# A hybrid diffusion layer on one core: casts bound behind other work, and unread products laid on TensorE

## The chip, the cores and the metric

The kernel runs on one core of a Trainium2 chip. Its engines are TensorE (PE; its weight loads are PEld), VectorE (DVE), ScalarE (ACT), GpSimd (POOL) and SyncE (SP), which issues most of the DMAs. Each engine works through its own queue in order; semaphores hold an instruction until what it reads is written and what it overwrites has been read. The metric is the device time of one execution in microseconds, as the median of several runs. All times here are microseconds.

## The reference

One layer with 512 latent tokens (x) and 256 context tokens (ctx), width 1024, all float32:

```python
def hybrid_layer(...):
    x = ffn_sublayer(x, mod_x, 0, ffn1_w_in, ffn1_w_out)        # SwiGLU, hidden 2816
    ctx = ffn_sublayer(ctx, mod_c, 0, ffn1_w_in, ffn1_w_out)
    qa, ka, va, qkv_b, z_b, a_b, b_b, ga, gb = split_proj(modulate(x, shift_x, scale_x) @ w_in)
    ...
    o_a = na_latent(grid(qa), grid(ka), grid(va), kc_h, vc_h, na_rpb)   # neighbourhood attention, 8 heads of 64
    o_ctx2, s_ctx = gated_delta_chunks(..., s0, update_ctx)             # gated DeltaNet, 4 heads of 128, both ways
    o_lat2, _ = gated_delta_chunks(..., s_ctx, True)
    o_b = gdn_output(o_lat2[0] + jnp.flip(o_lat2[1], axis=2), z_b, gdn_norm_w)
    y = sigmoid(ga) * (o_a @ w_pa) + sigmoid(gb) * (o_b @ w_pb)
    x = post_ln(DEEPNORM_ALPHA * x + gate_x * (y @ w_o), ln_g[1], ln_b[1])
    x = ffn_sublayer(x, mod_x, 2, ffn2_w_in, ffn2_w_out)
    return x
```

`ffn_sublayer` is a layer norm with a modulation, `(silu(a) * b) @ w_down` with `a, b = u @ w_up`, a gate and a layer norm behind it. The modulations come from `silu(c) @ w_ada`. The DeltaNet solves a triangular system for each chunk of 64 tokens and then carries a state from chunk to chunk.

## The kernel before

**Products.** Float32 is kept by splitting. Each weight tile of 128x1024 is copied by ScalarE into a high part of a shorter type (`S.copy`, L135, shown as CAST), and VectorE subtracts it to get the low part (L137); both are in `split`. Activations are split in the same way (uxh and uxl for x, uch and ucl for the context, oah and oal for what attention gives). One product is three matmuls: high by high, low by high and high by low (`mm3k`, L190 to L192; `down`, L209, for the second matrices). `Stream` (`ws` for most weights, `wso` for w_o) loads weight tiles ahead in the order of use and splits them; its dictionary `behind` can name, for the tile of a given number, two instructions behind which its cast and its subtraction are put.

**Order.** The kernel is built in program order, and a scheduler then orders each engine's queue by a simulated timeline (`schedule_with_timeline_sim=True`). `tc.issue_after(i)` binds the instructions made inside it to come after instruction `i` in the order. So a new instruction or a new bond can move others far away from it.

**PSUM.** TensorE writes to 8 banks. Pools name the places in them: in the first FFN the pool `pp1` has a ring "ps" of 8 places; then come `pm` (3 places) and `pg` (5), whose tiles lie on the same banks, later others. A tile on a bank waits until the last reader of the tile that was there has read it.

**Stages.** In order of time:
- Start (0 to about 40): the modulation columns are worked out by VectorE (L279) as the ada weights arrive; `modulate_k` (from L348) transposes the normed x for one block k of 128 columns (L360), and the first three FFN units add their products to six "acc" places (L413 to L415) as each k becomes ready. `spread_crow` (L290) lays the vector c over the partitions with two products ahead of that.
- First FFN, to about 607. Behind it `u2` (through `to_u`, L146 transposes, L149 reads) makes the modulated tokens; the context's second tile, `u2(fc, pp, "c", 1, ys[1])`, is the last work in pool `pp1`.
- w_in, to about 818: units that each make one projection (`units`), in pools `pm` and `pg`.
- DeltaNet, to about 1000: `grams(0)`, `grams(1)`, the block inverses `inv_of` (L857 products of 32x32 and 64x64 on T, which SyncE loads at L976 from the row that `base_inverse` wrote) and the scans. TensorE has fills from w_in beside them until these run out.
- Attention, to about 1095: four units m of two heads each, each of four blocks b (`attend`). A block is scores sc (L1240), softmax (VectorE, ScalarE's exponent at L1248, POOL's scaling of pr at L1251), transposes pt (L1255), ScalarE's copies pT (L1257) and the products po with the values (L1266). `att_load(p, m)` loads qa, ka and kc of unit m, casts them on ScalarE (L1169) and has POOL subtract (L1170). It is called for unit m+1 as unit m is made, and units m and m+2 share their places. Products with w_pb lie between.
- The gates (L1330 on): eight tiles of w_pa (`gated`), each followed by a gate and a split of yb into yh and yl; w_o's tiles are cast and subtracted meanwhile. Then w_o, and the second FFN: four units, each over half of the tokens in two passes (`for i in range(2)`), then products of half the size, and the end at 1528.8.

## Time and profile before

| | us |
|---|---|
| median of 3 runs | 1526.87 |
| the three runs | 1526.37 to 1531.96 |
| profiled execution | 1530.66 |
| its span | 1528.8 |
| TensorE busy in it | 1462.6 |
| VectorE busy | 1050.0 |
| ScalarE busy | 605.4 |
| POOL busy | 226.8 |

The profiled execution is one more execution with a recorder; its time is 1.9 us longer than its span. It lies 3.79 above the median of the runs, between the fastest and the slowest of the three. The mean granted clock of TensorE over the span is 0.988. In a row of the timeline the columns are the start, the time from the first instruction's start to the last one's end, the engine, line and operation, what it writes and reads, and in brackets the idle time of the engine just before and what ended it.

### The profile page before, as it was taken

The page shows a single profiled execution, that of the slowest core. Times are in us where ns is not written, and L with a number is a line of the kernel's source. Part 1 is how long each engine was busy: PE and PEld are TensorE (multiplying, and loading weights), DVE is VectorE, ACT ScalarE, POOL GpSimd, SP SyncE. Part 2 cuts the span into 40 slices and gives each one's busy share as a digit, 9 for nine tenths or more (in the row PEclk, how much of TensorE's full clock was granted, in tenths as well). Part 3 has the DMA queues.
Part 4 walks back from the last instruction along what each step waited for, and adds up shares of the span by engine and source line. Part 5 has one row for each costly group of instructions (what it writes and reads, how often), then busy time and mean ns, then how long its engine had stood idle before and what let it go on. Part 6 is the DMA issues. An engine that isn't in the chain of part 4 may idle for free.

```text
span 1528.8 us, 23646 instructions
## 1 busy us (share of the span) xinstructions
PE 1462.6 (96%) x9221; PEld 1258.7 (82%) x9221; DVE 1050.0 (69%) x1792; ACT 605.4 (40%) x1005; POOL 226.8 (15%) x224
## 2 busy tenths in 40 slices
PE   6999999999999999999996899999999999999997
PEld 4779988888888887889875778867678999998886
DVE  8765942597554587768777895576669699886426
ACT  5444221322222255546543444266416444344310
POOL 0000000000000011323301001366421022220001
PEclk9999999999999999999998999999999999999999
DMA  9665742667454334222476634283353143333422
GB/s 370 207 237 180 222 142 97 211 213 260 168 192 146 130 112 137 87 90 79 141 216 180 172 99 122 69 284 117 91 174 138 56 139 102 106 110 139 138 83 83
DMA packets 107586, 230.72 MB, mean 151 GB/s; under 512 B 34177, under 2 KB 47825, under 8 KB 107473
## 3 DMA queue, kind: packets, MB, share of 16 engines
q1 hardware_dynamic: 105312, 221.79, 44.7%
q10 hardware_dynamic: 1586, 5.32, 0.9%
q0 software_dynamic: 576, 2.10, 0.4%
q8 instruction: 72, 1.18, 0.3%
q14 instruction: 40, 0.33, 0.1%
HBM read 206.33 MB, written 22.85 MB: 150 GB/s over the span
## 4 chain that ended last, share of the span: by engine, by line
PE 76%; DVE 10%; DMA 7%; issue 3%; ACT 2%; POOL 2%; SPq 0%; DVEq 0%; ACTq 0%; POOLq 0%
PE ps L209 19%; PE ps L190 8%; PE ps L192 8%; PE ps L191 8%; PE pm L190 5%; PE pm L192 5%; PE pm L191 5%; PE pc L857 2%; PE ps L1478 2%; PE ps L1480 2%; PE ps L1479 2%; DVE wl L137 2%; PE po L1266 1%; DMA T<-rd 1%; PE pt L1255 1%
## 5 line engine op out<-in xcount | busy, mean ns | idle before, releaser
L137 DVE TENSOR_TENSOR wl<-wr,wh 128x1024 fp32r<-128x1024 f32 (+1 forms) x215 | 263.0, 1228 | 195.1 <-ACT wh L135 194.3
L135 ACT CAST wh<-wr 128x1024 fp32r<-128x1024 f32 (+1 forms) x215 | 217.8, 1018 | 333.4 <-PE ps L209 105.0
L192 PE MATMUL ps<-uxh,wl 128*128 128x512 f32 (+1 forms) x496 | 179.6, 363 | 2.2 <-DVE wl L137 2.2
L191 PE MATMUL ps<-uxl,wh 128*128 128x512 f32 (+1 forms) x496 | 179.3, 363 | 0.8 <-DVE uxl L137 0.8
L190 PE MATMUL ps<-uxh,wh 128*128 128x512 f32 (+1 forms) x496 | 179.6, 365 | 0.0
L279 DVE SCALAR_TENSOR_TENSOR adap<-wr,crow 128x1024 f32<-128x1024 f32 x112 | 136.8, 1221 | 38.5 <-DMA wr<-in_w_adaT_dram 37.1
L112 POOL TENSOR_TENSOR rs<-ve,mhalf 128x1 f32<-128x1 f32 (+2 forms) x46 | 50.4, 1099 | 744.6 <-DVE ve L108 735.4
L190 PE MATMUL pm<-uxh,wh 128*128 128x512 f32 x320 | 133.0, 416 | 4.1 <-ACT spill L609 2.1
L192 PE MATMUL pm<-uxh,wl 128*128 128x512 f32 x320 | 128.2, 401 | 0.7 <-DVE wl L137 0.7
L191 PE MATMUL pm<-uxl,wh 128*128 128x512 f32 x320 | 127.8, 399 | 0.0
L192 PEld LDWEIGHTS ps<-uxh,wl 128*128 128x128 f32 x496 | 93.7, 189 | 17.9 <-DVE wl L137 3.3
L191 PEld LDWEIGHTS ps<-uxl,wh 128*128 128x128 f32 x496 | 94.0, 189 | 14.9 <-DVE uxl L137 1.0
L190 PEld LDWEIGHTS ps<-uxh,wh 128*128 128x128 f32 x496 | 93.4, 189 | 14.3 <-issue 0.8
L190 PE MATMUL ps<-uch,wh 128*128 128x256 f32 x352 | 98.6, 280 | 0.0
L192 PE MATMUL ps<-uch,wl 128*128 128x256 f32 x352 | 98.3, 279 | 0.0
L191 PE MATMUL ps<-ucl,wh 128*128 128x256 f32 x352 | 98.2, 279 | 0.0
L209 PE MATMUL ps<-wh,hx 128*128 128x512 f32 x352 | 94.8, 389 | 0.0
L209 PEld LDWEIGHTS ps<-wh,hx 128*128 128x128 f32 x352 | 65.9, 188 | 13.6
L190 PEld LDWEIGHTS pm<-uxh,wh 128*128 128x128 f32 x320 | 61.6, 193 | 16.3 <-ACT spill L609 3.0
L192 PEld LDWEIGHTS pm<-uxh,wl 128*128 128x128 f32 x320 | 61.7, 193 | 14.8 <-DVE wl L137 1.5
L191 PEld LDWEIGHTS pm<-uxl,wh 128*128 128x128 f32 x320 | 61.6, 192 | 10.6
L190 PEld LDWEIGHTS ps<-uch,wh 128*128 128x128 f32 x352 | 66.1, 188 | 0.6
(411 smaller groups left out, 3438.7 us busy)
## 6 DMA issues: line engine op xcount, KB each, us to landing
wr<-in_w_adaT_dram SPq DMA_DIRECT2D x88, 512.0 KB, 4.7
wr<-in_up_dram SPq DMA_DIRECT2D x80, 512.0 KB, 4.2
wr<-in_dn_dram SPq DMA_DIRECT2D x58, 512.0 KB, 3.5
wr<-in_win_dram SPq DMA_DIRECT2D x52, 512.0 KB, 3.9
rb<-in_up_dram SPq DMA_DIRECT2D x18, 512.0 KB, 3.7
wr<-in_w_o_dram SPq DMA_DIRECT2D x8, 512.0 KB, 4.0
ac<-in_up_dram SPq DMA_DIRECT2D x6, 512.0 KB, 5.2
Dt<-gcd SPq DMA_DIRECT2D x12, 256.0 KB, 5.1
```

The lines of the kernel that those rows point to most:

```text
L112: G.tensor_tensor(rs[:], ve[:], mhalf[:, 0:n], ALU.pow)
L135: S.copy(hi, src)
L137: V.tensor_tensor(lo, src, hi.bitcast(F32), ALU.subtract)
L190: T.matmul(ps, a, uh[:, k, :], start=(k == 0), stop=False)
L191: T.matmul(ps, a, ul[:, k, :], start=False, stop=False)
L192: T.matmul(ps, b, uh[:, k, :], start=False, stop=(k == nk - 1))
L209: T.matmul(banks[t][d][:, c0:c1], a[:, sl], b[:, d * 512 + c0:d * 512 + c1], start=first and j == 0, stop=last and j == 2)
L279: V.scalar_tensor_tensor(pr[:], raw[:], 1.0, crow, op0=ALU.mult, op1=ALU.mult, accum_out=col[:, c:c + 1])
L857: last[0] = T.matmul(*a, **k).ins
L1478: T.matmul(ps[:], a, uh[:, k], start=k == 0, stop=False)
L1479: T.matmul(ps[:], a, ul[:, k], start=False, stop=False)
L1480: T.matmul(ps[:], b, uh[:, k], start=False, stop=k == 3)
```

## The change

It has six parts.
- `split` returns its two instructions, and `Stream` keeps those of its last tile (`last`). `mm3k` and `spread_crow` note their latest product in `marks["mm"]`. A new function `keep` makes n products that nobody reads, each bound behind a given instruction.
- Start: 26 such products of 128x512 on a tile of zeros (a place of the ring "hc", zeroed by POOL) into a place of the "acc" ring: 8 behind `spread_crow`, and 10, 5, 0 and 3 behind the first block's transposes of the four x tiles.
- One product of 64 columns into a new "ps" place, between the two `u2` of the context.
- Forty products of 128x512 into a "pc" place between `grams(1)` and the first `inv_of`.
- Attention: the casts of units 2 and 3 are bound behind the last copy pT of block 0 of the unit that was just made.
- In the gates' stage the cast and the subtraction of w_o's sixth tile are bound behind those of the last tile that `ws` had filled at m = 2; and ten products of 128x256 behind the last unit of the first pass of the second FFN.

```diff
     def split(src, hi, lo, behind=()):
         with tc.issue_after(behind[0]) if behind else nullcontext():
-            S.copy(hi, src)
+            a = S.copy(hi, src).ins
         with tc.issue_after(behind[1]) if behind else nullcontext():
-            V.tensor_tensor(lo, src, hi.bitcast(F32), ALU.subtract)
+            b = V.tensor_tensor(lo, src, hi.bitcast(F32), ALU.subtract).ins
+        return a, b
...
-                split(raw[:, 0:c], hi[:, 0:c], lo[:, 0:c], self.behind.get(self.i, ()))
+                self.last = split(raw[:, 0:c], hi[:, 0:c], lo[:, 0:c], self.behind.get(self.i, ()))
...
+    def keep(n, out, a, b, behind):
+        for _ in range(n):
+            with tc.issue_after(behind):
+                T.matmul(out, a, b, start=True, stop=True)
...
         for t, x_t in enumerate(xn[kind]):
-            T.transpose(ps[:, t * P:(t + 1) * P], x_t[:, k * P:(k + 1) * P], ident)
+            tr = T.transpose(ps[:, t * P:(t + 1) * P], x_t[:, k * P:(k + 1) * P], ident).ins
+            if kind == "x" and k == 0:
+                keep(KEEP[1 + t], wps[:], zero[:, 0:P], zero, tr)
...
+    KEEP = (8, 10, 5, 0, 3)
+    zero = tl(hcp, [P, 2, NCT], "hc", HF, F32R)[:].rearrange("p a n -> p (a n)")
+    G.memset(zero.bitcast(F32), 0.0)
+    wps = tl(pp0, [P, NX], "acc", 2 * F0)
     spread_crow(pp0, crow, 0)
+    keep(KEEP[0], wps[:], zero[:, 0:P], zero, marks["mm"])
...
     next(units[0])
+    keep(1, tl(pp, [P, 512], "ps", 8)[:, 0:64], uxh[:, 0, 0:P], uxh[:, 0, 0:64], marks["mm"])
     u2(fc, pp, "c", 1, ys[1])
...
     base = grams(1)
+    keep(40, tl(pgq, [P, 4, P], "pc", 2)[:].rearrange("p m c -> p (m c)"), uxh[:, 0, 0:P], uxh[:, 0, :], marks["mm"])
     inv_of(0, 0)
...
-    def att_load(p, m):
+    def att_load(p, m, behind=None):
...
-            S.copy(hi[:], lo[:].bitcast(F32))
+            with tc.issue_after(behind) if behind else nullcontext():
+                S.copy(hi[:], lo[:].bitcast(F32))
...
+    turned = {}
...
-                S.copy(pT[:], pt[:])
+                turned[b] = S.copy(pT[:], pt[:]).ins
...
-            ready = att_load((na_, ne)[m % 2], m + 1)
+            ready = att_load((na_, ne)[m % 2], m + 1, turned[0] if m else None)
...
         gt, ps = gated("pa", gad, m, oah, oal)
+        if m == 2:
+            wso.behind[5] = ws.last
...
             ffn_unit(lp, pp, *w0[f], uxh[:, :, sl], uxl[:, :, sl], 256, h[0][:, sl], h[1][:, sl])
+            if i == 0 and f == NH - 1:
+                keep(10, tl(pp, [P, 256], "ps", 8)[:], w0[f][0][0][:, 0:P], uxh[:, 0, sl], marks["mm"])
```

What the change does to the order shows at three places. The first is TensorE's queue at the end of pool `pp1`: last product of the unit in program order, the two halves of the transposes of the context's second tile y, and the first tile pm of the next pool (names carry a running number). Before:

```order
L191 MATMUL ps_973_5271<-uxl_787_4564,wh_938_5126 128x512
L192 MATMUL ps_973_5271<-uxh_786_4563,wl_939_5127 128x512
L146 MATMUL ps_976_5305<-ident_2_64,y1_961_5229 128x128 x4
L146 MATMUL ps_977_5316<-ident_2_64,y1_961_5229 128x128 x4
L190 MATMUL pm_981_5341<-uxh_786_4563,wh_953_5185 128x512
```

And with the change:

```order
L198 MATMUL ps_975_5300<-uxl_789_4593,wh_940_5155 128x512
L199 MATMUL ps_975_5300<-uxh_788_4592,wl_941_5156 128x512
L193 MATMUL ps_977_5333<-uxh_788_4592 128x64
L147 MATMUL ps_979_5336<-ident_2_64,y1_963_5258 128x128 x4
L147 MATMUL ps_980_5347<-ident_2_64,y1_963_5258 128x128 x4
L197 MATMUL pm_984_5372<-uxh_788_4592,wh_955_5214 128x512
```

The new product has a place of the ring; before, the first pm lay on the bank of ps_976, the first half of the transposes, and now it lies on the bank of ps_977, the product that nobody reads.

The second is ScalarE's queue in attention. Before, around the casts of unit 3 (kah_1874, qah_1872, kch_1876); pT_1774 and pT_1776 are the copies of block 0 of unit 1:

```order
L135 CAST oah_1692_9360<-oa_1742_9592 128x512
L1257 COPY pT_1774_9741<-pt_1773_9736 128x512
L1169 CAST kah_1874_10227<-ka_1875_10228 128x512
L1169 CAST qah_1872_10222<-qa_1873_10223 128x512
L135 CAST wh_1839_10054<-wr_1838_10052 128x512
L1169 CAST kch_1876_10232<-kc_1877_10233 128x256
L1257 COPY pT_1776_9748<-pt_1775_9743 128x512
```

With the change, around the casts of unit 3 (qah_1876, kah_1878, kch_1880); pT_1835 and pT_1837 are the copies of block 0 of unit 2:

```order
L1277 COPY pT_1835_10081<-pt_1834_10076 128x512
L135 CAST oah_1696_9432<-oa_1818_10022 128x512
L135 CAST wh_1892_10350<-wr_1891_10348 128x512
L1277 COPY pT_1837_10088<-pt_1836_10083 128x512
L1268 ACTIVATE pr_1856_10194,sm_1857_10195<-sc_1854_10178,nm_1855_10192 128x512 x2
L1187 CAST qah_1876_10294<-qa_1877_10295 128x512
L1187 CAST kah_1878_10299<-ka_1879_10300 128x512
L1187 CAST kch_1880_10304<-kc_1881_10305 128x256
```

The casts of unit 3 have moved from the copies of unit 1 to those of unit 2, and stand behind the exponents of one more block.

The third is TensorE's queue at the seam of the two passes of the second FFN. Before, the last product of the first pass and the first ones of the second:

```order
L192 MATMUL ps_2125_11461<-uxh_1996_10780,wl_2108_11246 128x256
L190 MATMUL ps_2127_11515<-uxh_1996_10780,wh_2086_11203 128x256
L190 MATMUL ps_2128_11516<-uxh_1996_10780,wh_2089_11209 128x256
L190 MATMUL ps_2132_11590<-uxh_1996_10780,wh_2092_11215 128x256
L190 MATMUL ps_2133_11591<-uxh_1996_10780,wh_2095_11221 128x256
L190 MATMUL ps_2135_11645<-uxh_1996_10780,wh_2098_11227 128x256
L190 MATMUL ps_2136_11646<-uxh_1996_10780,wh_2101_11233 128x256
L190 MATMUL ps_2138_11700<-uxh_1996_10780,wh_2104_11239 128x256
L191 MATMUL ps_2127_11515<-uxl_1997_10781,wh_2086_11203 128x256
```

With the change:

```order
L198 MATMUL ps_2129_11533<-uxl_2001_10853,wh_2111_11317 128x256
L199 MATMUL ps_2129_11533<-uxh_2000_10852,wl_2112_11318 128x256
L193 MATMUL ps_2131_11587<-uxh_2000_10852,wh_2108_11311 128x256 x10
L197 MATMUL ps_2132_11598<-uxh_2000_10852,wh_2090_11275 128x256
L198 MATMUL ps_2132_11598<-uxl_2001_10853,wh_2090_11275 128x256
```

Before, seven first products stood together ahead of the first one with uxl; now the ten products that nobody reads stand there, and the second pass goes on product by product.

## The prediction

> **What bounds the kernel now.** I read the page's busy times first, then the row of granted clocks and the chain of work that ended last, then the table by stretches of time, and last the timeline around each idle time of TensorE that an edit touches.

> ```profile
> PE 1462.6 (96%) x9221; PEld 1258.7 (82%) x9221; DVE 1050.0 (69%) x1792; ACT 605.4 (40%) x1005; POOL 226.8 (15%) x224
> PEclk9999999999999999999998999999999999999999
> PE 76%; DVE 10%; DMA 7%; issue 3%; ACT 2%; POOL 2%; SPq 0%; DVEq 0%; ACTq 0%; POOLq 0%
> ```

> TensorE is busy for 1462.6 us of the span of 1528.8, so about 66 us of idle time and whatever the clock loses are all that such edits can win. The clock row is near full everywhere. What it hides shows in slices of one microsecond (columns: window, sum, busy PE, PEld, DVE, ACT, POOL with counts, granted clock, DMA share, GB/s):

> ```profile
> 610.00:611.00 1.00, 0.44 (x2) 0.36 (x3) 0.00 (x0) 1.00 (x4) 0.00 (x0) 0.92 0.31 37
> 614.00:615.00 1.00, 1.00 (x6) 0.82 (x5) 1.00 (x2) 0.83 (x1) 0.00 (x0) 0.87 0.07 16
> 836.00:837.00 1.00, 1.00 (x5) 0.81 (x5) 1.00 (x2) 0.00 (x0) 0.00 (x0) 0.94 0.26 104
> 1040.00:1041.00 1.00, 1.00 (x5) 0.41 (x3) 0.97 (x2) 0.39 (x1) 0.00 (x0) 0.54 0.00 0
> ```

> ```profile
> 607.43:610.84 3.41, 1.49 (x11) 1.16 (x10) 1.24 (x2) 3.27 (x8) 0.00 (x0) 1.00 0.01 5
> 860.01:863.43 3.42, 1.73 (x10) 1.31 (x8) 3.35 (x9) 2.42 (x6) 0.00 (x0) 1.00 0.30 108
> 935.11:938.52 3.41, 1.70 (x42) 1.45 (x42) 1.63 (x6) 2.97 (x9) 1.57 (x4) 1.00 0.34 119
> 1030.68:1034.09 3.41, 1.53 (x11) 0.88 (x9) 1.08 (x3) 1.81 (x4) 1.14 (x1) 1.00 1.00 361
> 1034.09:1037.51 3.42, 2.63 (x18) 2.28 (x18) 1.45 (x3) 3.29 (x10) 3.39 (x4) 0.50 0.39 127
> 1184.28:1187.69 3.41, 1.28 (x11) 1.29 (x12) 2.52 (x3) 2.66 (x4) 0.00 (x0) 1.00 0.37 114
> ```

> Stretches with 1.28 to 1.70 us of PE work were followed by one at half clock; the one with 1.73 wasn't. A stretch at half clock does 1.71 us of work less. So a gap of g us costs g itself, and where over about 1.7 us of it lie in one stretch, 1.71 us more: for g between 1.7 and 3.41, laid anywhere on the grid, that has a chance of about g/3.41, and a shorter gap alone costs no fall. The next stretch stays at half where the gap reaches into it; at 1034.09 it did so with 2.63 us busy, much of it transposes.

> **The change part by part.** The sum is made against the profiled execution (1530.66 us, span 1528.8); its falls are worth less in the median (1526.87, 3.79 below), since another execution meets the grid elsewhere. I give both.

> *The ring place* (one product of 64 columns ahead of the second half of the context's transposes).

> ```profile
> 607.60 1.03 PE L146 MATMUL ps<-ident,y 128*128 128x128 f32 x8
> 609.00 2.90 ACT L149 ACTIVATE u<-ps,colc 128x128 f32<-128x128 f32 x8
> 610.56 0.58 PE L190 MATMUL pm<-uxh,wh 128*128 128x512 f32 x1 [1.92 <-ACT u L149]
> ```

> The first tile of the next pool lies on the bank of the first half of these transposes, which ScalarE must read in full first. In the changed order the bank is that of the unread product, and the transposes lie on banks of the small pool. The wait of 1.92 us goes, and the fall at 610.84 (1.71) with it: −3.6 in this execution, −1.92 − 0.56 × 1.71 = −2.9 on average. What could be late next is any other wait of TensorE, and there is none for 148 us:

> ```profile
> 615.00:763.00 148.00, 148.00 (x928) 132.43 (x927) 108.45 (x177) 78.16 (x128) 44.67 (x45) 1.00 0.31 99
> ```

> So what is won is carried on to 763. The product itself, a quarter of the columns of the last FFN's 0.115 us (below), is under 0.1 us. Bounds: 0 and −3.6.

> *Forty products before the first inverse.*

> ```profile
> 817.64 0.39 PE L192 MATMUL pm<-uxh,wl 128*128 128x512 f32 x1
> 818.32 0.39 PE L192 MATMUL pm<-uxh,wl 128*128 128x512 f32 x1
> 826.42 2.02 SPq L976 DMA_DIRECT2D T<-rd  x4
> 831.15 0.68 PE L857 MATMUL pi<-T,Bt 32*32 32x32 f32 x32 [12.44 <-DMA T<-rd]
> ```

> From the first of these rows to the second are three products, 0.68 us, 0.227 each; forty take about 9.1 us and fill 818.7 to 827.8 of a gap of 12.44 whose end is set by SyncE's loads of T; nobody waits for the forty, and no queue but TensorE's gets longer. They leave 831.15 − 827.8 = 3.35 us idle, which nearly always takes one stretch below 1.7 us of work. Before, the clock was at half for the 4.97 us of work from 831.15 to 836.12 (2.5 lost); after, for one stretch (1.71): −0.8 here. On average the restart lost about 1.7 (half a stretch, and half the time one more) and will lose about 1.4, as part of the stretch at half then lies in the gap: −0.3. Bounds: −2.5 (no fall left) and +1.0 (the loads come earlier than the forty end).

> [...]

> *Attention's casts.*

> ```profile
> 1032.25 0.62 ACT L1169 CAST kah<-ka 128x512 fp32r<-128x512 f32 x1 [4.01 <-DMA ka<-kad]
> 1033.94 0.40 ACT L1169 CAST kch<-kc 128x256 fp32r<-128x256 f32 x1
> 1034.25 0.58 ACT L1257 COPY pT<-pt 128x512 f32<-128x512 f32 x1
> 1034.88 0.90 PE L1266 MATMUL po<-pT,vw 128*64 128x128 f32 x5 [1.88 <-ACT pT L1257]
> ```

> ScalarE stands 4.01 us for the load of ka of unit 3, whose cast stands ahead of a copy of unit 1 that TensorE needs. The change puts the casts of units 2 and 3 behind the copies of block 0 of the unit before. So 1.88 us go, and here two stretches at half clock (3.41 of work): −5.3; on average −1.88 − 1.5 = −3.4 (a chance of 0.55, of one or two stretches). Against it stands what comes later: the casts and POOL's subtractions behind them.

> ```profile
> 1018.03 1.27 POOL L1170 TENSOR_TENSOR ka<-ka,kah 128x512 fp32r<-128x512 f32 x1
> 1019.27 0.72 POOL L1170 TENSOR_TENSOR kc<-kc,kch 128x256 fp32r<-128x256 f32 x1
> 1019.96 1.26 POOL L1170 TENSOR_TENSOR qa<-qa,qah 128x512 fp32r<-128x512 f32 x1
> 1042.98 3.10 POOL L1251 TENSOR_SCALAR pr<-pr,sm 128x512 f32<-128x512 f32 x2 [3.27 <-DVE sm L1249]
> 1056.27 0.60 PE L1255 MATMUL pt<-ident,pr 128*128 128x128 f32 x4
> 1060.02 0.39 PE L1240 MATMUL sc<-kah,qah 64*128 64x256 f32 x2
> ```

> The last transposes of unit 2's block 0 are at 1056.27 and unit 3's first scores at 1060.02. Copy (0.58), casts (0.62, 0.62 for qa of the same size, 0.40) and subtractions (3.25) behind the transposes (0.60) make 6.1 us against 3.75. That is 2.3 us too late. The changed order softens it: it lays transposes and products of unit 2 between the scores with ka's high part and those with its low part. I take +1.0 for what remains, between 0 and the 2.3. Together −4.3 here, −2.4 on average; bounds −5.3 and +3.

> *The cast of w_o's sixth tile, bound behind the last cast of the weight w_pa.*

> ```profile
> 1101.42 0.50 PE L192 MATMUL pm<-oah,wl 128*128 128x512 f32 x1 [0.95 <-DVE wl L137]
> 1112.38 1.75 DVE L137 TENSOR_TENSOR wl<-wr,wh 128x512 fp32r<-128x512 f32 x1
> 1114.18 0.50 PE L192 MATMUL pm<-oah,wl 128*128 128x512 f32 x1 [1.78 <-DVE wl L137]
> ```

> TensorE waits for VectorE's low parts 0.95 and 1.78 us. VectorE's changed order has one of w_o's two subtractions, and later a yl, behind w_pa's. A subtraction of 128x512 is about 0.7 us, so each wait can lose that, 1.4 together, but VectorE is full here and something else is then late: I take −1.2, bounds 0 and −2.7.

> *Ten products between the passes of the last FFN.*

> ```profile
> 1194.29 0.28 PE L191 MATMUL ps<-uxl,wh 128*128 128x256 f32 x1
> 1194.40 0.28 PE L192 MATMUL ps<-uxh,wl 128*128 128x256 f32 x1
> 1194.52 0.98 PE L190 MATMUL ps<-uxh,wh 128*128 128x256 f32 x7
> ```

> The next pass starts at 1194.52 without a wait, so there is no gap for them: +10 × 0.115 = +1.2. The gap that lets the clock fall at 1187.69 (1.28 us busy in the stretch before) lies ahead of that and stays. Bounds 0 and +1.2.

> *Twenty-six products at the start.*

> ```profile
> 27.02 0.68 DVE L137 TENSOR_TENSOR uxl<-fs,uxh 128x512 fp32r<-128x512 f32 x1
> 27.76 0.50 PE L414 MATMUL acc<-uxl,wh 128*128 128x512 f32 x1
> 20.00:40.00 20.00, 20.00 (x89) 15.63 (x89) 19.97 (x39) 10.88 (x14) 0.00 (x0) 1.00 0.98 365
> ```

> A clock that is up earlier can win one stretch at half, 1.7 us, for the products before 24 us. But VectorE is busy 19.97 of 20 us and TensorE's product at 27.76 starts as its subtraction ends, so it would wait there instead: 0, bounds −1.7 and +0.4 (a transpose pushed back by the products ahead of it).

> Sum here: −3.6 − 0.8 − 4.3 − 1.2 + 1.2 + 0 = −8.7, so 1522.0 from 1530.66. Average: −2.9 − 0.3 − 2.4 − 1.2 + 1.2 + 0 = −5.6, so 1521.3 from the median. I take **1521** us. The rest of the reordering (inverses, pass two of the last FFN) I cost at nothing, ±3.

> **The rivals.** *More of the clock is won:* the start counts (−1.7), the stretch at half after the forty isn't there either (−1.7), and the scores come in time (−1.0): 1521.3 − 4.4, about 1517. For it: each fall here has a gap of its own; against it VectorE's 19.97 of 20. [...] *The attention gain is given back:* with the casts later, all of the reordering of units 1 to 3 makes new waits of their own size: +2.3 and up to +3 more, 1524 to 1527. For it: the changed rows there are many, and POOL's scaling of pr now stands ahead of the subtractions. *Slower:* in units 2 and 3 POOL reaches its subtractions only behind a scaling of pr (3.10 in the row above) and ends them after TensorE has run out of other work. Each time up to 2.3 + 3.1 = 5.4 us idle and a fall or two, 2 × (5.4 + 1.7) = 14.2; less the 3.4 for the wait for ka and the 3.2 won elsewhere this gives 1526.9 + 14.2 − 3.4 − 3.2, about 1534.5, and 1538 where each fall lasts two stretches. It decides where POOL's subtraction ends over 5 us after the first score. *Not what it says:* the ring place doesn't move the bank; then 1524, within the forecast's range and counted in its chance.

> **How the numbers follow.** Forecast, 1517 to 1525: 0.44 (0.15 of it below 1519.2). More clock: 0.22 (0.20 below). Only wholly idle stretches: 0.05 (0.03 below). Given back: 0.20, all within. Slower: 0.09 (0.06 of it above 1534.5). 0.5%, 7.6 us, is about what a measurement of this kernel can tell from no change. Faster 0.38, same 0.56, slower 0.06. The range goes from 1513, the more-clock case with w_o's bound (−1.5) and 2.5 of the unseen reordering, to 1528, the given-back case with 1 us of the unseen reordering.

> **What would show it.** Right: no wait for u at the first pm tile and a granted clock of 1.00 from 600 to 780; in the gap near 818 forty rows of 128x512 and at most one stretch at 0.50 after it; ScalarE without a wait of 4 us for ka; ten rows of 128x256 that start without a wait before them. The forecast is wrong if waits of TensorE for the scores' low parts in units 2 and 3 add up to over 3 us, if the 26 products shorten the time to the first pass of FFN1's end, or if the stages without an edit (40 to 600, 1200 to 1500) differ by over 2 us.

## The result, and the profile after

The changed kernel takes **1542.27 us** (median of 6 runs, 1540.75 to 1544.23) against 1528.3 for the kernel before, run beside it on the same chip (1526.37 to 1531.96). The ratio is 1.009, with an interval of 1.0077 to 1.0103: 14.0 us slower. The forecast was 1521, its range ended at 1528, and the slowest rival on record at 1538. In the experiments below one execution of e1 took 3630 us and one of g1 2251 us, both far slower than their others; the medians of these two kernels are given without them.

The page of the changed kernel, its rows on busy times and the chain that ended last:

```profile
PE 1484.0 (96%) x9298; PEld 1276.2 (83%) x9298; DVE 1049.7 (68%) x1792; ACT 606.4 (39%) x1005; POOL 229.1 (15%) x225
PE 73%; DVE 13%; DMA 6%; issue 3%; POOL 2%; ACT 1%; SPq 1%; DVEq 0%; POOLq 0%; ACTq 0%
```

TensorE is idle for 56.4 us, 9.8 less than before, and yet the span ends 11.6 later, at 1540.4: its busy time has grown by 21.4. Busy time is no gain by itself here, since products that nobody reads count in it. The chain has lost 3 points of TensorE and got 3 of VectorE, so more of the end is set by somebody whom TensorE waits for. The list of TensorE's waits says who (columns: what waits, for whom, us in total, times, the longest):

```profile
PE pi L873 <- DMA T<-rd: 7.0, 3, 4.7
PE ps L297 <- DVE fs L279: 4.6, 1, 4.6
...
PE pt L1242 <- ACT pT L1277: 2.8, 2, 2.5
```

The wait for T has shrunk to 7.0 from 13.0 in the same list of the kernel before, as the forty products lie in it. The second row isn't in that list, and the last stands there with 0.3 in total. The wait for fs is early, in the first FFN; here is the second `spread_crow` in TensorE's timeline of the changed kernel, and the product behind it:

```profile
62.04 3.78 PE L297 MATMUL ps<-crow,one_row 1*128 1x512 f32 x4 [4.57 <-DVE fs L279]
65.74 0.80 PE L197 MATMUL ps<-uxh,wh 128*128 128x512 f32 x1
```

and of the kernel before:

```profile
57.37 1.98 PE L290 MATMUL ps<-crow,one_row 1*128 1x512 f32 x4
```

Before, it follows the first units without a wait. Now it stands 4.57 us until VectorE has read the last of the units' sums (`fs`, started at 61.29, 0.69 long):

```profile
61.29 0.69 DVE L279 TENSOR_TENSOR fs<-fs,acc 128x512 f32<-128x512 f32 x1 [0.26 <-ACT fs L278]
```

Where the wait comes from: in the program's allocation a pool's rings have their places in the order in which their first tiles are made, and bank 0 belonged to the small ring "ps" before. The unread products' place of the ring "acc" is now the first tile of its pool, so that ring has bank 0 for its first place; the sixth sum of the units lies there, and the next pool's first tile, that of `spread_crow`, lies on bank 0 too. The stretches of the clock's grid there (columns as in the prediction's tables by stretches):

```profile
58.07:61.48 3.41, 0.00 (x0) 0.00 (x0) 3.07 (x5) 1.45 (x3) 0.00 (x0) 1.00 0.86 288
61.48:64.90 3.42, 2.86 (x4) 1.16 (x4) 1.19 (x2) 1.22 (x2) 0.00 (x0) 0.50 0.34 134
64.90:68.31 3.41, 3.41 (x8) 2.08 (x7) 1.80 (x3) 0.60 (x1) 0.00 (x0) 0.50 0.00 0
68.31:71.72 3.41, 3.41 (x9) 2.64 (x9) 3.38 (x10) 0.00 (x0) 0.00 (x0) 0.50 0.74 216
```

A wait of 4.57 and three stretches at half clock: from equal at 57 the changed kernel is about 9 us behind when the clock returns at 71.72. At 96 it gets 1.9 us of that back: there the kernel before waits 1.91 us for a low part that is now ready.

At the end of `pp1` the ring place does what it is for:

```profile
614.01 0.19 PE L193 MATMUL ps<-uxh 128*128 128x64 f32 x1
614.04 1.07 PE L147 MATMUL ps<-ident,y 128*128 128x128 f32 x8
614.86 0.48 PE L197 MATMUL pm<-uxh,wh 128*128 128x512 f32 x1
```

The first pm tile starts without the wait for u, and the clock doesn't fall (1.00 from 71.72 to 832.89). Against the kernel before this wins 3.7 us from 610 to 614.

The gap before the first inverse, TensorE's timeline and the stretches around it:

```profile
819.38 9.23 PE L193 MATMUL pc<-uxh 128*128 128x512 f32 x40
833.36 0.69 PE L873 MATMUL pi<-T,Bt 32*32 32x32 f32 x32 [4.75 <-DMA T<-rd]
```

```profile
829.48:832.89 3.41, 0.00 (x0) 0.00 (x0) 1.44 (x8) 0.00 (x0) 0.89 (x5) 1.00 1.02 259
832.89:836.30 3.41, 2.94 (x38) 2.38 (x38) 3.13 (x14) 1.61 (x4) 2.38 (x5) 0.50 0.26 60
836.30:839.72 3.42, 2.11 (x36) 1.35 (x35) 3.15 (x12) 1.54 (x2) 1.46 (x4) 0.50 0.45 153
839.72:843.13 3.41, 3.41 (x9) 2.64 (x9) 3.27 (x9) 0.00 (x0) 0.00 (x0) 0.50 0.00 0
```

The products fill what they were to fill, but the rest of the gap, 4.75 us, has a whole stretch in it, and the clock stays at half for the three stretches after it (9.77 us from 833.36).

In attention ScalarE no longer stands 4 us for ka. Its timeline around the casts of unit 3, and two of TensorE's rows:

```profile
1067.49 0.62 ACT L1187 CAST qah<-qa 128x512 fp32r<-128x512 f32 x1
1068.00 0.63 ACT L1187 CAST kah<-ka 128x512 fp32r<-128x512 f32 x1
1068.52 0.42 ACT L1187 CAST kch<-kc 128x256 fp32r<-128x256 f32 x1
1068.83 2.00 ACT L135 CAST wh<-wr 128x1024 fp32r<-128x1024 f32 x2
1070.72 1.08 ACT L1277 COPY pT<-pt 128x512 f32<-128x512 f32 x2
```

```profile
1018.62 1.97 PE L1242 MATMUL pt<-ident,vst 128*128 128x128 f32 x8 [2.46 <-ACT pT L1277]
1071.37 0.43 PE L1286 MATMUL po<-pT,vw 128*64 128x128 f32 x2 [1.80 <-ACT pT L1277]
```

The casts and two of weight tiles stand ahead of copies pT; TensorE waits 1.80 for the first of these, about as long as the 1.88 that were taken away. The 2.46 at 1018.62 are for a copy behind the casts of unit 2.

### The profile page after: what moved, and what is told of

It is laid out like the page before. It is cut to its first block, busy times and chain, and to the rows that moved or that the text cites. A ratio compares the mean times of both kernels' runs of the same rounds, so it can differ in the third digit from the quotient of the medians.

```text
span 1540.4 us, 23799 instructions
## 1 busy us (share of the span) xinstructions
PE 1484.0 (96%) x9298; PEld 1276.2 (83%) x9298; DVE 1049.7 (68%) x1792; ACT 606.4 (39%) x1005; POOL 229.1 (15%) x225
## 4 chain that ended last, share of the span: by engine, by line
PE 73%; DVE 13%; DMA 6%; issue 3%; POOL 2%; ACT 1%; SPq 1%; DVEq 0%; POOLq 0%; ACTq 0%
PE ps L216 19%; PE ps L197 9%; PE ps L199 9%; PE ps L198 9%; PE pm L197 5%; PE pm L199 5%; PE pm L198 5%; DVE wl L137 2%; PE pc L873 2%; PE po L1286 1%; PE ps L1504 1%; PE ps L1506 1%; PE pt L1275 1%; PE ps L1505 1%; DVE Xt L971 1%
## 5 line engine op out<-in xcount | busy, mean ns | idle before, releaser
L137 DVE TENSOR_TENSOR wl<-wr,wh 128x1024 fp32r<-128x1024 f32 (+1 forms) x215 | 261.5, 1220 | 195.6 <-ACT wh L135 194.6
```

The source lines that it names most:

```text
L137: b = V.tensor_tensor(lo, src, hi.bitcast(F32), ALU.subtract).ins
```

## Experiments

Seventeen runs, in five sets; those of one set share the runs of the kernel before (medians 1527.2, 1527.19, 1527.07, 1527.52, 1527.54). "Cost" is the median less that of the kernel before.

| run | median | ratio to before, interval | cost |
|---|---|---|---|
| a1 change, place moved | 1537.29 | 1.0055 [1.0036, 1.0073] | +10.1 |
| a2 change, one product at the start | 1537.89 | 1.0064 [1.0043, 1.0086] | +10.7 |
| b1 ring place alone | 1525.48 | 0.9981 [0.9972, 0.9991] | −1.7 |
| b2 forty alone | 1536.91 | 1.0061 [1.0036, 1.0086] | +9.7 |
| a0 the change again | 1540.1 | 1.0073 [1.0056, 1.009] | +12.9 |
| b2s thirty-two in place of forty | 1533.22 | 1.0034 [1.002, 1.0048] | +6.0 |
| b3 attention's casts alone | 1531.93 | 1.0025 [1.0013, 1.0037] | +4.7 |
| b4 w_o's bond alone | 1524.73 | 0.9981 [0.9967, 0.9994] | −2.5 |
| b5 ten alone | 1527.46 | 1.0 [0.9989, 1.0011] | +0.4 |
| e1 forty short ones, old order | 1529.15 | 1.0012 [0.9998, 1.0026] | +2.1 |
| e2 fifty short ones, new order | 1533.56 | 1.0049 [1.0032, 1.0066] | +6.5 |
| d2 ring, w_o, start with its place moved | 1522.39 | 0.9967 [0.9955, 0.9979] | −4.7 |
| g1 stores on ScalarE's queue | 1541.9 | 1.009 [1.0066, 1.0114] | +14.4 |
| g2 g1 with forty | 1540.77 | 1.0079 [1.0062, 1.0097] | +13.3 |
| g3 d2 with g1's stores | 1530.63 | 1.0016 [0.9999, 1.0033] | +3.1 |
| h1 chain's DMAs on POOL's queue | 1538.45 | 1.008 [1.006, 1.01] | +10.9 |
| h2 h1 with forty | 1541.6 | 1.0098 [1.0078, 1.0117] | +14.1 |

### The start

**The place** (the changed kernel; on every engine the order stays as it was):

```diff
-    wps = tl(pp0, [P, NX], "acc", 2 * F0)
     spread_crow(pp0, crow, 0)
+    wps = tl(pp0, [P, NX], "acc", 2 * F0)
```

> The changed kernel with one line moved: the place in the acc ring for the start's unread products is taken behind spread_crow and no longer ahead of it; every engine's order stays the same. Theory P (the place): the first tile of the next pool stood on the bank of the last GLU's input, read by VectorE at 62 us; with the move it stands on a bank of the ps ring again. The 4.6 us wait and the 10.2 us at half clock behind it go, and of the 9.1 us that they cost 1.9 were won back at 96 us, so 7 us less than the changed kernel: about 1535. Theory R (the products, or the zero tile): nothing changes, 1542.

```profile
57.35 1.98 PE L297 MATMUL ps<-crow,one_row 1*128 1x512 f32 x4
```

With the small ring's places made first the wait is gone, as in the kernel before. That settles what the wait comes from. The median is 2.8 below that of the change's second set of runs (1540.1) and 5.0 below the first (1542.27). If that is the price of the place, it is a third to a half of the 9.1 that are lost at 62, and the rest is got back on the way, at 96 and in later waits that are there anyway (below, the ring place).

**The products** (the changed kernel):

```diff
-    KEEP = (8, 10, 5, 0, 3)
+    KEEP = (1, 0, 0, 0, 0)
```

> The changed kernel with 1 unread product at the start where it has 26; the place in the acc ring is taken as before, ahead of spread_crow. Theory P (the place): the wait of 4.6 us stays, 1542. Theory R (the products): about 1535. For the start itself both expect no change by 48 us.

```profile
61.95 3.77 PE L297 MATMUL ps<-crow,one_row 1*128 1x512 f32 x4 [4.57 <-DVE fs L279]
```

The wait stays with one product, so it is the place and not the products that makes it. Without 25 of the 26 the kernel isn't slower (1537.89 against 1540.1): they win nothing. But a2, with the wait, is as fast as a1, without it (1537.89 and 1537.29), and came at neither of the two times forecast for it (1542 and 1535). So what the wait costs at the end is not shown: 2.8 to 5.0 by a1, next to nothing by a2.

### The parts alone

**The ring place** on the kernel before; the one product is all that is added, and no other row moves:

```diff
+    keep(1, tl(pp, [P, 512], "ps", 8)[:, 0:64], uxh[:, 0, 0:P], uxh[:, 0, 0:64], marks["mm"])
     u2(fc, pp, "c", 1, ys[1])
```

> The kernel before with the ring place's one product alone; every other row of every engine's order is the same. The prediction's term: 1.9 us of wait and on average half a fall less, -2.9, 1525.4 against 1528.3. Rival (absorbed): what is won at 610 is lost again between 763 and 831, where VectorE, ScalarE and the loads set the pace: 0, 1528.3.

1.7 of the 2.9 arrive. In the trace 3.59 are won at 613; then the wait for T, which SyncE's loads and VectorE set, takes a part back. It was 12.44 us before:

```profile
829.23 0.71 PE L866 MATMUL pi<-T,Bt 32*32 32x32 f32 x32 [15.28 <-DMA T<-rd]
```

At 831 of the kernel before, 1.92 of the 3.59 are left. About half of what was won ahead of this wait counts at the end. That the loss at the start is halved in the same way is not shown.

**The forty** on the kernel before, with the products of 512 columns as in the change:

```diff
     base = grams(1)
+    keep(40, tl(pgq, [P, 4, P], "pc", 2)[:].rearrange("p m c -> p (m c)"), uxh[:, 0, 0:P], uxh[:, 0, :], marks["mm"])
     inv_of(0, 0)
```

> The kernel before with the forty products ahead of the first inverse alone (the scheduler moves some 90 rows of TensorE and 180 of VectorE behind them). The prediction's term: -0.3, 1528. Rival (restart and new order): the rest of the gap lets the clock fall as before, it returns only after a stretch that is busy throughout, 10 us at half instead of 5, and the DeltaNet stage loses 3 to 6 us by its new order: 1532 to 1535.

The dearest part: +9.7, more than the rival on record allowed. That rival had the clock return only behind a stretch that is busy throughout, as it does at all 13 returns from 61 to 1202 us in the traces of the kernel before (614.26 the first) and of the changed kernel (71.72 the first). In b2 it returned behind a stretch with 2.94 us busy (833.79, in the last section). To get from the one order to the other at least 65 rows of TensorE, 93 of VectorE, 25 of ScalarE, 17 of SyncE and 4 of POOL have to change places, most of them from the DeltaNet to attention.

**The change again, thirty-two, the casts, w_o's bond, the ten.** The edits: none; `keep(32, ...)` for `keep(40, ...)`; `turned[0] if m else None` in `att_load`'s call alone; `wso.behind[5] = ws.last` alone; `keep(10, ...)` alone.

> The changed kernel once more, on the same chip as the runs beside it. With one unread product at the start in place of 26 the wait of 4.6 us stayed and the time was 1537.9, 4.4 below what the changed kernel gave on another chip. Theory P (the place, not the products): the two have the same time where they run on the same chip, so 1538 to 1540 here. Theory R (the products cost 4 us somewhere): 1542.

> The kernel before with 32 products in the gap where the run b2_forty has 40. The work is nearly the same (7.3 us against 9.1, all inside the gap of 12.4), but the scheduler moves 46 rows of TensorE behind them in place of 91, and none of POOL. Theory O (the order): what b2_forty lost, about 5 us between the restart and 950 and 2 to 3 in attention, comes from its new order, and most of it isn't here: 1527 to 1531. Rival G (the products in the gap, by their clock or by the later end of the loads of T): as b2_forty, 1535 to 1537.

> The kernel before with attention's casts bound alone. The prediction's term: -2.4, 1524.8 (from 1527.2). Rival (given back): the wait of 1.9 us for ka goes, but the casts and what stands behind them now hold a copy pT or the scores of units 2 and 3, 0 to +3: 1527 to 1530.

> The kernel before with the cast of w_o's sixth tile bound alone. The prediction's term: -1.2, 1526. Rival (moved, not removed): TensorE's waits for w_pa's low parts keep their sum of 2.7 us, and the new order in the second FFN adds or takes up to 2: 1526 to 1529.

> The kernel before with the ten products between the passes of the last FFN alone. The prediction's term: +1.2, 1528.4; what the parts measured so far leave for it: within 1 of nothing. Rival (order): seven first products of the second pass no longer stand together, and 20 rows of ScalarE move; 0 to +3.

Thirty-two still cost 6.0, between the two forecasts. Their order differs from that of the kernel before in the DeltaNet alone, in SyncE's queue too. The casts alone lose 4.7, more than either forecast. Their trace has these waits in TensorE's timeline, and two rows of ScalarE's behind the last two of them:

```profile
1056.26 0.43 PE L1276 MATMUL po<-pT,vw 128*64 128x128 f32 x2 [1.80 <-ACT pT L1267]
1068.37 0.58 PE L1250 MATMUL sc<-kah,qah 64*128 64x256 f32 x2 [2.14 <-ACT pr L1258]
1101.55 0.50 PE L197 MATMUL pm<-oah,wh 128*128 128x512 f32 x1 [2.98 <-ACT wh L135]
...
1066.87 0.69 ACT L1258 ACTIVATE pr<-sc,nm 128x512 f32<-128x512 f32 x1 [1.66 <-DVE nm L1254]
1099.93 2.09 ACT L135 CAST wh<-wr 128x1024 fp32r<-128x1024 f32 x3 [3.74 <-DMA wr<-in_w_o_dram]
```

All three are for ScalarE: a copy behind the casts, an exponent, and a weight's cast in the gates that is late. Only the first is for work behind the moved casts; ahead of the exponent ScalarE itself waits 1.66 for VectorE's maximum nm, and ahead of the weight's cast 3.74 for the load of a tile of w_o. These two come with the new order. None of the three is for POOL's subtractions; the waits for these add up to 0.5 (0.2 in the kernel before). From 990 to 1115 all of TensorE's waits add up to 14.9 against 11.3 in the kernel before, where those for w_pa's low parts are longer (2.7 against 0.2). The clock is at half from 1068.35 to 1071.76 and from 1102.48 to 1105.90.

w_o's bond wins 2.5, more than either forecast, yet the waits that it was to shorten are still there, 0.96 and 1.88 at 1094.79 and 1108.32 of its trace, and most of the TensorE rows that it moves lie in the second FFN. Where it wins is open. The ten products cost 1.17 in the changed kernel's timeline (1205.38 to 1206.55) and nothing that the runs can tell (+0.4, interval −1.7 to +1.7).

### What of the forty costs: the products or the order

Two kernels with shorter products, on the kernel before: forty of 96 columns, with which no other row of any engine moves (e1), and fifty of 64 columns, with which the order becomes nearly that of the forty (e2; the same line with 50 and 64):

```diff
+    keep(40, tl(pgq, [P, 4, P], "pc", 2)[:].rearrange("p m c -> p (m c)")[:, 0:96], uxh[:, 0, 0:P], uxh[:, 0, 0:96], marks["mm"])
```

> The kernel before with 40 products of 96 columns in the gap, short enough for the scheduler: no other row of any engine moves. They should take 3 to 5 us of the gap of 12.4. Theory O (the order): no change, 1526 to 1528. Rival G (products in the gap do the harm, by the clock or by what they delay): some part of b2_forty's +9.7, 1530 to 1534.

> The kernel before with 50 products of 64 columns in the gap: about the same work as e1_old_order, but the scheduler now gives nearly the order that it gave with forty of 512 columns (TensorE's rows, POOL's and SyncE's but two the same; 18 of VectorE's and 2 of ScalarE's differ). Theory O: as b2_forty, 1533 to 1538, with the loss between the restart at 831 and 950 and some in attention. Rival G: as e1_old_order.

e2's fifty products take 6.26 us, and its wait before the inverse stays 9.48 us long. With the old order the short products cost 2.1, between the two forecasts, and with the new one 6.5. No trace shows the stages of e1. In the trace of e2 the second inverse is late: it is equal to the kernel before at 831, and 3.72 behind at 882. SyncE's queue, in the kernel before and in the changed kernel:

```profile
871.89 1.50 SPq L947 DMA_DIRECT2D L<-bd  x2
873.49 2.68 SPq L959 DMA_DIRECT2D rd<-Xt  x4
876.26 0.56 SPq L613 DMA_DIRECT2D gad<-spill  x1
876.92 0.39 SPq L172 DMA_DIRECT2D wr<-in_win_dram  x1
877.49 2.11 SPq L976 DMA_DIRECT2D T<-rd  x4
```

```profile
875.97 0.30 SPq L963 DMA_DIRECT2D L<-bd  x1
876.37 0.52 SPq L627 DMA_DIRECT2D gad<-spill  x1
876.93 0.42 SPq L963 DMA_DIRECT2D L<-bd  x1
877.66 0.45 SPq L173 DMA_DIRECT2D wr<-in_win_dram  x1
878.25 4.17 SPq L975 DMA_DIRECT2D rd<-Xt  x4
884.68 0.94 SPq L992 DMA_DIRECT2D T<-rd  x2
```

A store of a gate's input (gad) now stands between the two loads of L, and T comes 7.2 us later, 2.2 of it from before the first inverse. The theory was then that these stores hold the loads up. So they were given ScalarE's queue, behind the tanh that writes their data, without the forty (g1), with them (g2), and in the best version (g3):

```diff
-        nc.sync.dma_start(dst[m], t[:])
+        (nc.scalar if name in ("ga", "gb") else nc.sync).dma_start(dst[m], t[:])
```

> The kernel before with one change: the stores of the gates' inputs (gad and gbd from spill) are issued on ScalarE's queue, right behind the tanh that writes the spill, and no longer on SyncE's. It is the base for the next run. Both theories: 1522 to 1530, within 4 of the kernel before, as no wait of TensorE in the kernel before is put down to these stores. Read on the row of the second inverse's loads of T (877.49 in the kernel before).

> The same with the forty products of 512 columns before the first inverse. Alone on the kernel before they cost 9.7. Theory Q (SyncE's queue): most of that comes from stores of gad and gbd that the new order puts between SyncE's loads of L and T, where they wait for ScalarE. With the stores on ScalarE's queue nothing stands there but loads of weights, so forty costs 0 to +4 against the run before this one. Rival C (the products themselves, the clock after them, and VectorE's new order): the stores are beside the point and forty still costs 7 to 11.

> The version that has beaten both kernels (ring place, w_o's bond, start's products with their place behind the crow's products; 1522.39), with the stores of gad and gbd on ScalarE's queue as in the two runs before. If the queue is free of cost or gain: 1520 to 1525, 3 to 6 below the first run of this call.

As a base g1 was to be harmless and costs 14.4; g3 is 8.2 above d2. Forty on top of g1 cost nothing (−1.1); 19 rows of VectorE, 7 of ScalarE and one each of SyncE and POOL change places with them. The theory of the stores falls: in g1 they are gone from SyncE's queue, and a load of a weight stands ahead of L there.

```profile
876.27 0.35 SPq L172 DMA_DIRECT2D wr<-in_win_dram  x1
877.59 0.91 SPq L947 DMA_DIRECT2D L<-bd  x2
```

L comes 5.7 us later than in the kernel before, where the first inverse was 1.7 later. So the DMAs of the inverses' chain themselves were given a queue of their own, POOL's, without and with the forty; from the one to the other no other row of any engine moves. The edit for L and Ltr; those for rd (L959) and T (L976) are alike:

```diff
-            nc.sync.dma_start(dst, bass.AP(bd.tensor, bd.offset + (q // 2) * 8 * MSTR, [[st, 32], [P, 32], [1, 32]]))
+            nc.gpsimd.dma_start(dst, bass.AP(bd.tensor, bd.offset + (q // 2) * 8 * MSTR, [[st, 32], [P, 32], [1, 32]]))
```

> The kernel before with one change: the DMAs of the inverses' chain (L and Ltr from bd, rd from Xt, T from rd) are issued on POOL's queue in place of SyncE's, so no store of a gate's input and no load of a weight stands among them. It is the base for the next run. If such neighbours on SyncE hold up the second inverse in some orders only, this base is within 4 of the kernel before or, where POOL's queue is slower to issue, up to 10 above it; no claim rests on that. What is read: the start of the second inverse after the first, 51.1 in the kernel before (831.15 to 882.25).

> The same with the forty products of 512 columns before the first inverse. In this form they are the one row that is added, and no other row of any engine moves. Theory R (the price of forty is the order that it makes): against the run before this one they cost -2 to +2.5. Theory C (the products, or the clock behind them, cost time by themselves): they cost 6 to 11, as they do on the kernel before (9.7).

TensorE's timelines of h1 and of h2, the first products of the first and the second inverse:

```profile
830.83 0.65 PE L857 MATMUL pi<-T,Bt 32*32 32x32 f32 x32 [16.85 <-DMA T<-rd]
...
890.62 0.45 PE L857 MATMUL pi<-T,Bt 32*32 32x32 f32 x32
```

```profile
812.49 9.23 PE L193 MATMUL pc<-uxh 128*128 128x512 f32 x40
828.98 0.65 PE L864 MATMUL pi<-T,Bt 32*32 32x32 f32 x32 [7.26 <-DMA T<-rd]
...
890.67 0.45 PE L864 MATMUL pi<-T,Bt 32*32 32x32 f32 x32
```

With all forty products in the gap the second inverse starts within 0.05 us of where it starts without them; counted from the first inverse, as the expectation reads it, that is 61.69 us against 59.79. The three pairs in which (nearly) no other row moves give +2.1 (e1), −1.1 (g2 less g1) and +3.2 (h2 less h1), and by the ratios' intervals none of them is told from zero. The +3.2 lies between the two forecasts (up to 2.5, from 6). On the kernel before, where the order moves, forty cost 9.7. So by these medians the greater part of the price is the order. g1 and h1 lose as much without one product, h1 0.9 more than the 10 that its expectation allowed. But a queue differs in them as well as the order: two loads of Ltr take 1.58 us on POOL's queue in h1 and 0.93 on SyncE's in the kernel before.

All traces in one table, by whether the DeltaNet has the order of the kernel before (times from the first inverse's first product to the second's, and to the first product with oah, where the gates begin):

| | to the second inverse | to the gates |
|---|---|---|
| order as before: before, b1, b3, b4, b5, d2 | 50.7 to 52.7 | 256.7 to 263.5 (263.5 is b3) |
| another order, no forty: g1, h1, g3 | 53.3 to 59.8 | 265.1 to 272.1 |
| another order, unread products: b2, b2s, e2, g2, h2 | 53.0 to 61.7 | 266.3 to 269.3 |
| the change: after, a0, a1, a2 | 55.0 to 56.3 | 267.1 to 271.5 |

No kernel with another order has a shorter time in either column than any with the old one. Each of these times is of one execution, and a queue differs in the second group and products are added in the third and fourth, so the table alone doesn't tell the order's part; the pairs above do. Which row of the order is to blame stays open: neither the stores alone (g1) nor SyncE's queue as a whole (h1) could be cleared away so that the stage was as fast as before, since each such edit moves other rows again.

### The best version

d2 is the kernel before with the ring place, w_o's bond and the start's products, their place made behind `spread_crow`; no forty, no casts, no ten.

> The parts that won alone: the ring place and the cast of w_o's sixth tile, and the 26 products at the start with their place taken behind spread_crow. Without forty, attention's bonds and ten. If the parts add up (-1.7, -2.5, and 0 for the start): 1523.0. If the start's products win what the clock lost before 24 us: 1521.5. If gains ahead of 763 are lost again before 831 in full: 1524.7.

At 1522.39 it is below both kernels (0.9967 of the kernel before, interval 0.9955 to 0.9979), 4.7 us, about what the ring place and w_o's bond win alone (1.7 + 2.5). The start's products need not be in it.

## Why the prediction was wrong

The parts alone, and the start's place (a0 less a1, +2.8), sum to −1.7 + 9.7 + 4.7 − 2.5 + 0.4 + 2.8 = +13.4; the change costs 12.9 and 14.0 in its two sets of runs. So the parts account for the whole, as far as intervals of 1.5 to 3.8 us either way for a part can tell; the prediction had −5.6 for the same sum. Point by point:

- **The step that failed most**: "The rest of the reordering (inverses, pass two of the last FFN) I cost at nothing, ±3", and with it, for the forty, that "no queue but TensorE's gets longer". The new product lies in a gap of TensorE, but the scheduler orders the other engines around it. That order makes the greater part of the 9.7: 6.5, if the products' own price is the largest of the three pairs' (3.2), and with short products 4.4 (e2 less e1). Which row of it does so stays open. I had looked at the gap alone, and not at what SyncE's and VectorE's queues had become by the second inverse.
- **The forty's own term**, −0.3 with bounds −2.5 and +1.0. The gap's rest was to be 3.35 and is 4.75; the clock was to be at half for one stretch and is for three (two in b2). And the clock there is worth less than I took: from the first inverse's first product to its first 64x64 product on Y it takes 13.7 us in the kernel before, b1, a1 and d2, with the clock at half for 3.3 to 5.0 us of it, so TensorE's clock doesn't set this piece (in the kernel before TensorE waits 0.70 us for VectorE's Y at its end). Only the 8.5 to 9.8 us at half of after, a0 and a2 lengthened it, by 1.6 to 2.2. That only wholly idle stretches are followed by a fall, which had a chance of 0.05, no run shows: in the kernel before it fell behind stretches with 1.28 to 1.70 us busy, and in the changed kernel behind one with 2.01.
- **Attention**, −2.4 with bounds −5.3 and +3: it costs 4.7. The mechanism on record as "given back" is right, and larger than the +2.9 that it allowed (−2.4 + 5.3): in b3 the new waits (1.80, 2.14, 2.98) are 6.9, with two falls. I looked for the later price in POOL's subtractions, on which the rival "slower" rested; the waits for them come to 0.5. Against the 1.88 that were won stand 1.80 for a copy behind the moved casts; the other two are of the new order, which I hadn't costed, and end with VectorE (nm) and a load of w_o.
- **The start**, 0 with bounds −1.7 and +0.4. That the 26 products win nothing is right. The products before 24 us did run faster with them: they start 0.43 us apart from 22.37 to 23.65 in the kernel before, and 0.23 to 0.24 apart from 22.11 to 22.82 in the changed kernel. Yet the product that waits for VectorE's uxl starts at 27.75 there and at 27.76 in the kernel before, as the prediction had it. But only the products were costed, not the ring place that they take: it made TensorE wait 4.57 us for VectorE at 62. What that costs at the end is open (2.8 to 5.0 by a1, next to nothing by a2).
- **The ring place**: mechanism right to the row (no wait for u, clock at 1.00, bank as said), −2.9 forecast, −1.7 measured. Too large, since "what is won is carried on to 763" doesn't hold beyond it: the wait for T takes half back.
- **w_o's cast**: −1.2, bounds 0 and −2.7; −2.5 measured, though not by the waits that I named, so that it lies within the bounds is luck.
- **The ten**: +1.2; 1.17 in the trace, +0.4 in the median.

The signs of a wrong forecast that the prediction named were nearly right: it looked for waits of over 3 us in attention for POOL (what grew are the waits for ScalarE's copies pT, 6.9 in sum against 4.3) and for differences in stages without an edit. The first such stage, 57 to 72, is where the trace first departs.

## What to carry to other kernels

Where a scheduler orders all queues, an instruction that is put into a gap is costed by the new order of every engine up to the next stage, DMA queues first, and not by the gap: forty products cost 9.7 here where the order moved, and −1.1 to +3.2 where (nearly) no other row did. A pair of kernels that differ in the inserted work alone tells the two prices apart. A filler's PSUM place is part of it: made ahead of the others, it turned a ring by a bank here, and in the next pool TensorE waited 4.57 us for the reader of an earlier tile. Its width is part of it too: while the forty products of 512 columns ran (819.38 to 828.61) the granted clock was 1.00, and behind a stretch full of the fifty of 64 it fell (820.35 in e2, below). What a fall of the clock costs is read from the stage that it lies in: the restart above took 13.7 us with 3.3 of it at half and with 5.0. And of the 3.59 us that were won ahead of the wait for T, which ends with a DMA, 1.92 were left behind it.

## What the hardware showed beyond that

In these traces the busy time of a stretch, as the rows give it, doesn't tell whether the clock falls or returns behind it. Five stretches of the grid, in order from b4 (two), the changed kernel, b2 and a2:

```profile
56.83:60.24 3.41, 3.41 (x11) 1.64 (x11) 3.41 (x4) 2.03 (x4) 0.00 (x0) 1.00 0.70 185
858.96:862.37 3.41, 1.49 (x9) 1.12 (x7) 3.34 (x9) 2.64 (x6) 0.00 (x0) 1.00 0.32 87
945.53:948.94 3.41, 2.01 (x42) 1.67 (x43) 3.00 (x9) 2.97 (x9) 2.55 (x5) 1.00 0.33 78
833.79:837.21 3.42, 2.94 (x13) 1.82 (x6) 3.18 (x13) 1.86 (x4) 3.08 (x7) 0.50 0.26 78
1067.95:1071.37 3.42, 3.42 (x20) 2.21 (x18) 1.23 (x3) 2.27 (x5) 3.42 (x3) 0.50 0.81 261
```

Behind the first the clock fell, though TensorE was busy throughout (3.41 us). The four products of one row that `spread_crow` makes (1 partition of 128, 1.98 us) lie wholly in it, as they do in such stretches of four more traces (b2s, b5, g3, h2), each followed by a fall. In the kernel before a border at 57.88 divides them, and in d2 one at 59.42 cuts off their last 0.06 us; no fall follows there. So in these seven traces a fall follows where all four lie in one stretch; why is not shown. In e2 the clock fell at 820.35, behind a stretch full of the fifty products of 64 columns. Behind the second row it didn't fall, with 1.49 us busy, and behind the third it did, with 2.01, products of 32x32 among them; so the 1.70 us of the prediction's rows are no border. The clock returned behind the fourth row, with 2.94 busy, and not behind the fifth, with 3.42. So here a return didn't need a stretch that is busy throughout, and didn't always follow one. In the changed kernel the stretch from 64.90 was busy throughout too (3.41), until 65.82 with the last of the products of one row, and the clock stayed at half for one more, three in all behind one gap (61.48 to 71.72). What decides a fall or a return is not shown.
